# Huber loss on one core: two rows per partition in pair slots in place of one row per slot

## The chip, the cores and the metric

The kernel runs on one core of one Trainium2 chip. The time is device microseconds of one execution. Before was timed three times. One execution was taken with the hardware profiler, and all durations below are from it.

## The reference

```python
# pred, target: (8192, 8192) float32
diff = pred - target
abs_diff = np.abs(diff)
out = np.where(abs_diff <= 1.0, 0.5 * diff**2, abs_diff - 0.5)
```

It is elementwise: 256 MiB of `pred` and 256 MiB of `target` are read, 256 MiB are written, and each output element depends on one element of either input. Both kernels use the same identity: with d the difference and c the difference clamped to [0, 1] (of |d|) or [-1, 1] (of d), the result is max(|d| - 0.5, c * c / 2).

## The kernel before

The 8192 rows are cut into 64 blocks of 128 rows. A block's row p lies in partition p, so that each partition holds one whole row of 8192 float32 values, 32 KiB. Six slots of 128 x 8192 are the whole of the working memory (192 KiB in each partition), and no slot belongs to one tensor: `free` and `spent` are lists of slot numbers. A block takes one slot `a` for pred and one slot `b` for target. The result is written over the target (`b`); the pred slot is spent as soon as the block's last instruction has read it, and the target slot when its store has landed.

All loads and stores are issued from SP, in the order of the program, and a DMA that must wait for its slot holds up all that stand behind it. In steady state the order is: pred of block i (L66, into a spent slot), target of block i (L68, into the slot whose store has to land first), store of block i-2 (L73).

Five instructions compute a block. VectorE (DVE) subtracts (`sub`, L41), ScalarE (ACT) takes the absolute value in place (`absolute`, L49), DVE clamps it into the target's slot (`clamp`, L44), ACT squares that and halves it (`half_square`, L52), and DVE joins both with a maximum (`finish`, L55). The finish of a block is issued after the subtraction of the next one (`waiting`, `settle`). The last four blocks (`FINE`) are computed in four pieces of 2048 columns, and the last block's target load and the last store are cut in the same way.

The order of instructions on every engine is the one in which the program writes them (`tc.manual_schedule()`); waits follow from the tiles' data.

Of the kernel before, what the change touches and what calls it, by code (L numbers as in the profile page):

```python
# [1 line left out]

# [4 lines left out]


@with_exitstack
def kernel(  # L10
    ctx: ExitStack,
    tc: tile.TileContext,
    pred: bass.AP,
    target: bass.AP,
    out: bass.AP,
):
    nc = tc.nc
    P = 128
    fp32 = mybir.dt.float32
    Alu = mybir.AluOpType  # L20
    Act = mybir.ActivationFunctionType
    SQRT_HALF = 0.70710678118654752

    n_rows, W = pred.shape
    pred_t = pred.rearrange("(n p) m -> n p m", p=P)
    targ_t = target.rearrange("(n p) m -> n p m", p=P)
    out_t = out.rearrange("(n p) m -> n p m", p=P)
    n = pred_t.shape[0]

    NSLOT = 6  # L30
    PIECES = 4
    FINE = 4

    pool = ctx.enter_context(tc.tile_pool(name="slots", bufs=1))
    slots = [pool.tile([P, W], fp32, name=f"slot{k}") for k in range(NSLOT)]
    free = list(range(NSLOT))
    spent = []
    pending = []

    def sub(a, b):  # L40
        nc.vector.tensor_tensor(out=a, in0=a, in1=b, op=Alu.subtract)  # L41

    def clamp(a, b):
        nc.vector.tensor_scalar(  # L44
            out=b, in0=a, scalar1=0.0, scalar2=1.0, op0=Alu.max, op1=Alu.min
        )

    def absolute(a):
        nc.scalar.activation(out=a, in_=a, func=Act.Abs)  # L49

    def half_square(b):
        nc.scalar.activation(out=b, in_=b, func=Act.Square, scale=SQRT_HALF)  # L52

    def finish(a, b):
        nc.vector.scalar_tensor_tensor(  # L55
            out=b, in0=a, scalar=-0.5, in1=b, op0=Alu.add, op1=Alu.max
        )

    def cuts(pieces):
        w = W // pieces  # L60
        return [slice(k * w, (k + 1) * w) for k in range(pieces)]

    def load(i):
        ia = spent.pop(0) if i >= 3 else free.pop(0)
        ib = free.pop(0) if free else spent.pop(0)
        nc.sync.dma_start(out=slots[ia], in_=pred_t[i, :, :])  # L66
        for c in cuts(PIECES if i == n - 1 else 1):
            nc.sync.dma_start(out=slots[ib][:, c], in_=targ_t[i, :, c])  # L68
        return ia, ib

    def store(i, ib):
        for c in cuts(PIECES if i == n - 1 else 1):
            nc.sync.dma_start(out=out_t[i, :, c], in_=slots[ib][:, c])  # L73
        free.append(ib)

    ctx.enter_context(tc.manual_schedule())

    waiting = []

    def settle(keep):  # L80
        while len(waiting) > keep:
            finish(*waiting.pop(0))

    def compute(a, b, pieces):
        lag = 1 if pieces == 1 else 2
        if pieces > 1:
            while waiting and waiting[0][0].shape[1] == W:
                finish(*waiting.pop(0))
        for c in cuts(pieces):
            sub(a[:, c], b[:, c])  # L90
            absolute(a[:, c])
            settle(lag - 1)
            clamp(a[:, c], b[:, c])
            half_square(b[:, c])
            waiting.append((a[:, c], b[:, c]))

    for i in range(n):
        ia, ib = load(i)
        if i >= 2 and i < n - 1:
            store(*pending.pop(0))  # L100
        spent.append(ia)
        pending.append((i, ib))
        compute(slots[ia], slots[ib], PIECES if i >= n - FINE else 1)
    settle(0)
    for p in pending:
        store(*p)


# [1 line left out]
_INS = ['pred', 'target']  # L110
_OUTS = [((8192, 8192), 'float32')]


# [23 lines left out]
```

## Time and profile before

| | |
|---|---|
| median of 3 runs | 1873.06 us (1871.8 to 1877.19) |
| profiled execution, its own time | 1873.31 us |
| its span | 1871.5 us |
| DVE busy | 1386.8 us (74%), 228 instructions |
| ACT busy | 906.0 us (48%), 153 instructions |
| DMA packets, bytes | 28517, 805.36 MB, mean 430 GB/s |
| target load of 4 MiB, issue to landing (median) | 19.3 us |
| store of 4 MiB, issue to landing (median) | 21.4 us |
| pred load of 4 MiB, issue to landing (median) | 30.6 us |

The span runs from the first to the last event of the profiled execution; 1.8 us of the execution's own time lie around it. "Issue to landing" counts from the DMA instruction on SP to the arrival of its last byte, so it holds the time that the transfer spent in the queue behind earlier ones. In the busy tenths each digit is one of 40 equal slices of the span (46.8 us each), and 9 stands for 90% or more.

### The profile page before, as it was taken

Reading aid. Unit: us, or ns where it says so; the run is one execution under the profiler, and the core shown is the slowest. Engines: PE = TensorE matmul, PEld = TensorE weight load, DVE = VectorE, ACT = ScalarE, POOL = GpSimd, SP = SyncE. Lnnn points to the kernel's source line nnn. Section 1 sums busy time; section 2 is a strip of 40 time slices with the busy share of each in tenths; the row PEclk is TensorE's granted clock in tenths of the full one; section 3 lists DMA queues with packets and bytes.
Section 4 is the critical chain, followed back from the end, with each engine's and each line's share of the span. In section 5 each row is a group of like instructions: output and inputs, shape, how many; then the busy total and the mean of one; then the engine's idle time right before and its main releaser. Section 6 shows DMA issues by size and latency. Waiting matters only on the chain.

```text
span 1871.5 us, 823 instructions
## 1 busy us (share of the span) xinstructions
DVE 1386.8 (74%) x228; ACT 906.0 (48%) x153; POOL 0.2 (0%) x4
## 2 busy tenths in 40 slices
DVE  3886776868678687686776867768678686686787
ACT  2644545444454444544545445444454444544555
POOL 0000000000000000000000000000000000000000
DMA  9999999999999999999999999999999999999998
GB/s 415 415 432 431 432 432 429 434 426 430 435 431 434 434 431 434 433 432 434 432 432 435 431 434 432 433 434 433 432 433 434 431 435 431 434 433 432 434 434 382
DMA packets 28517, 805.36 MB, mean 430 GB/s; under 512 B 3168, under 2 KB 3168, under 8 KB 3168
## 3 DMA queue, kind: packets, MB, share of 16 engines
q1 hardware_dynamic: 28512, 805.32, 100.0%
q14 instruction: 5, 0.04, 0.0%
HBM read 536.87 MB, written 268.44 MB: 430 GB/s over the span
## 4 chain that ended last, share of the span: by engine, by line
DMA 68%; DVE 31%; ACT 0%; issue 0%; DVEq 0%; SPq 0%
DMA out_dram<-slot 35%; DMA slot<-in_target_dram 32%; DVE slot L41 15%; DVE slot L55 15%; DVE slot L44 1%; ACT slot L49 0%; DVEq L132 0%; DVEq L41 0%; SPq L66 0%; SPq L68 0%; DVEq L44 0%; SPq L73 0%
## 5 line engine op out<-in xcount | busy, mean ns | idle before, releaser
L41 DVE TENSOR_TENSOR slot<-slot,slot 128x8192 f32<-128x8192 f32 (+1 forms) x76 | 558.1, 7343 | 456.2 <-DMA slot<-in_target_dram 456.2
L49 ACT ACTIVATE slot<-slot 128x8192 f32<-128x8192 f32 (+1 forms) x76 | 452.4, 5952 | 576.3 <-DVE slot L41 576.3
L52 ACT ACTIVATE slot<-slot 128x8192 f32<-128x8192 f32 (+1 forms) x76 | 452.3, 5951 | 375.7 <-DVE slot L44 375.7
L55 DVE SCALAR_TENSOR_TENSOR slot<-slot,slot 128x8192 f32<-128x8192 f32 (+1 forms) x76 | 557.5, 7337 | 7.1 <-ACT slot L52 7.1
L44 DVE TENSOR_SCALAR slot<-slot 128x8192 f32<-128x8192 f32 (+1 forms) x76 | 284.8, 3747 | 11.0 <-ACT slot L49 11.0
L49 ACT ACT_TABLE_LOAD x1 | 1.3, 1283 | 0.7 <-PEq L121 0.7
L121 POOL MEMSET const-bfloat16-1.0<- 128x1 bf16 x1 | 0.1, 101 | 0.0
L121 POOL MEMSET const-uint8-127<- 128x1 uint8 x1 | 0.1, 101 | 0.0
L121 POOL MEMSET const-float32-0.0<- 128x1 f32 x1 | 0.1, 98 | 0.2 <-issue 0.2
L121 POOL MEMSET const-float32-1.0<- 128x1 f32 x1 | 0.1, 98 | 0.0
## 6 DMA issues: line engine op xcount, KB each, us to landing
slot<-in_pred_dram SPq DMA_DIRECT2D x64, 4096.0 KB, 30.6
slot<-in_target_dram SPq DMA_DIRECT2D x63, 4096.0 KB, 19.3
out_dram<-slot SPq DMA_DIRECT2D x63, 4096.0 KB, 21.4
slot<-in_target_dram SPq DMA_DIRECT2D x4, 1024.0 KB, 15.2
out_dram<-slot SPq DMA_DIRECT2D x4, 1024.0 KB, 9.8
```

The source lines that it names most:

```text
L41: nc.vector.tensor_tensor(out=a, in0=a, in1=b, op=Alu.subtract)
L44: nc.vector.tensor_scalar(out=b, in0=a, scalar1=0.0, scalar2=1.0, op0=Alu.max, op1=Alu.min)
L49: nc.scalar.activation(out=a, in_=a, func=Act.Abs)
L52: nc.scalar.activation(out=b, in_=b, func=Act.Square, scale=SQRT_HALF)
L55: nc.vector.scalar_tensor_tensor(out=b, in0=a, scalar=-0.5, in1=b, op0=Alu.add, op1=Alu.max)
L121: nc = _bacc.Bacc("TRN2", target_bir_lowering=False, num_devices=1)
```

## The change

A block is now 256 rows, and each partition holds two neighbouring rows of it, which lie next to each other in memory: 64 KiB. There are 32 such blocks. The same 192 KiB in each partition are laid out as two pair slots of 64 KiB (`pairs`), which alternate from block to block, and two row slots of 32 KiB (`rows`). A pair slot takes both rows of pred in one load, is computed in place, and is stored in one store. A row slot takes one row of the target: slot 0 the even rows, slot 1 the odd rows.

The order on SP in one period is: store of pair i-1, odd target row of block i, pair i+1 of pred, even target row of block i+1. The odd target row and the store both wait for the computation of block i-1's odd rows; the next pair waits for the store of the pair that had its slot; the even target row waits for the computation of block i's even rows.

A row is computed in pieces: two of 4096 columns (even), 4096, 2048 and 2048 (odd), and four of 2048 for the last block. Within a piece DVE subtracts and clamps to [-1, 1] one after the other, ACT squares and then takes the absolute value, and DVE's finish follows up to two pieces later (and writes over pred's place, not the target's). A row's pieces are all finished before the next row begins. The five operations are the same in number per element as before.

The first block's even row is loaded in four DMAs of 2 MiB, and pred's odd row of the first block and both pred rows of the last block are loaded one by one. The last block's odd target row and odd output row go in four pieces of 1 MiB.

```diff
-    NSLOT = 6
-    PIECES = 4
-    FINE = 4
-    slots = [pool.tile([P, W], fp32, name=f"slot{k}") for k in range(NSLOT)]
+    R = 2
+    pred_t = pred.rearrange("(n p r) m -> n p (r m)", p=P, r=R)
+    targ_t = target.rearrange("(n p r) m -> n p (r m)", p=P, r=R)
+    out_t = out.rearrange("(n p r) m -> n p (r m)", p=P, r=R)
+    pairs = [pool.tile([P, R * W], fp32, name=f"pair{k}") for k in range(2)]
+    rows = [pool.tile([P, W], fp32, name=f"row{k}") for k in range(R)]
+    EVEN = [4096, 4096]
+    ODD = [4096, 2048, 2048]
+    FINE = [2048, 2048, 2048, 2048]
...
+    def load_pair(i):
+        nc.sync.dma_start(out=pairs[i % 2], in_=pred_t[i, :, :])
+    def load_row(i, r, widths=None):
+        for c in cuts(widths or [W]):
+            nc.sync.dma_start(out=rows[r][:, c], in_=targ_t[i, :, at_row(r, c)])
+    def store_pair(i):
+        nc.sync.dma_start(out=out_t[i, :, :], in_=pairs[i % 2])
...
+        for c in cuts(widths):
+            a, b = pairs[i % 2][:, at_row(r, c)], rows[r][:, c]
+            nc.vector.tensor_tensor(out=a, in0=a, in1=b, op=Alu.subtract)
+            nc.vector.tensor_scalar(
+                out=b, in0=a, scalar1=-1.0, scalar2=1.0, op0=Alu.max, op1=Alu.min
+            )
+            nc.scalar.activation(out=b, in_=b, func=Act.Square, scale=SQRT_HALF)
+            nc.scalar.activation(out=a, in_=a, func=Act.Abs)
+            todo.append((a, b))
+            finish(2)
+        finish(0)
...
-    for i in range(n):
-        ia, ib = load(i)
-        if i >= 2 and i < n - 1:
-            store(*pending.pop(0))
-        spent.append(ia)
-        pending.append((i, ib))
-        compute(slots[ia], slots[ib], PIECES if i >= n - FINE else 1)
-    settle(0)
-    for p in pending:
-        store(*p)
+    for c in cuts(EVEN):
+        nc.sync.dma_start(out=pairs[0][:, c], in_=pred_t[0, :, c])
+        nc.sync.dma_start(out=rows[0][:, c], in_=targ_t[0, :, c])
+    load_pred_row(0, 1)
+    for i in range(n):
+        last = i == n - 1
+        if not last:
+            load_row(i, 1)
+            if i + 1 < n - 1:
+                load_pair(i + 1)
+            else:
+                load_pred_row(i + 1, 0)
+        compute(i, 0, EVEN if not last else FINE)
+        if not last:
+            load_row(i + 1, 0)
+        compute(i, 1, ODD if not last else FINE)
+        if i + 1 == n - 1:
+            load_pred_row(i + 1, 1)
+            load_row(i + 1, 1, FINE)
+        if not last:
+            store_pair(i)
+    store_row(n - 1, 0, [W])
+    store_row(n - 1, 1, FINE)
```

More of the change, by code (lines that the diff above doesn't have):

```diff
@@ L24 @@
     n_rows, W = pred.shape
-    pred_t = pred.rearrange("(n p) m -> n p m", p=P)
-    targ_t = target.rearrange("(n p) m -> n p m", p=P)
-    out_t = out.rearrange("(n p) m -> n p m", p=P)
+    pred_t = pred.rearrange("(n p r) m -> n p (r m)", p=P, r=R)
+    targ_t = target.rearrange("(n p r) m -> n p (r m)", p=P, r=R)
+    out_t = out.rearrange("(n p r) m -> n p (r m)", p=P, r=R)
     n = pred_t.shape[0]
-    NSLOT = 6
-    PIECES = 4
-    FINE = 4
     pool = ctx.enter_context(tc.tile_pool(name="slots", bufs=1))
-    slots = [pool.tile([P, W], fp32, name=f"slot{k}") for k in range(NSLOT)]
@@ L36 @@
[L36 to L74, printed above, removed]
@@ L76 @@
-    ctx.enter_context(tc.manual_schedule())
[L78 to L95, printed above, removed]
@@ new lines, with cuts, at_row, load_pred_row @@
+    FINE = [2048, 2048, 2048, 2048]
+    def cuts(widths):
+        out_, at = [], 0
+        for w in widths:
+            out_.append(slice(at, at + w))
+            at += w
+        return out_
+    def at_row(r, c):
+        return slice(r * W + c.start, r * W + c.stop)
+    def load_pair(i):
+        nc.sync.dma_start(out=pairs[i % 2], in_=pred_t[i, :, :])
+    def load_pred_row(i, r):
+        c = slice(r * W, (r + 1) * W)
+        nc.sync.dma_start(out=pairs[i % 2][:, c], in_=pred_t[i, :, c])
@@ new lines, in load_row, with store_row, compute, finish @@
+    def load_row(i, r, widths=None):
[3 more added lines that the diff above has]
+        nc.sync.dma_start(out=out_t[i, :, :], in_=pairs[i % 2])
+    def store_row(i, r, widths):
+        for c in cuts(widths):
+            ca = at_row(r, c)
+            nc.sync.dma_start(out=out_t[i, :, ca], in_=pairs[i % 2][:, ca])
+    def compute(i, r, widths):
+        todo = []
+        def finish(keep):
+            while len(todo) > keep:
+                a, b = todo.pop(0)
+                nc.vector.scalar_tensor_tensor(
+                    out=a, in0=a, scalar=-0.5, in1=b, op0=Alu.add, op1=Alu.max
+                )
+        for c in cuts(widths):
+            a, b = pairs[i % 2][:, at_row(r, c)], rows[r][:, c]
+            nc.vector.tensor_tensor(out=a, in0=a, in1=b, op=Alu.subtract)
+            nc.vector.tensor_scalar(
+                out=b, in0=a, scalar1=-1.0, scalar2=1.0, op0=Alu.max, op1=Alu.min
+            )
+            nc.scalar.activation(out=b, in_=b, func=Act.Square, scale=SQRT_HALF)
[3 more added lines that the diff above has]
+        finish(0)
```

## The prediction, made before the changed kernel ran

> **What bounds the kernel now.** I read the page first: busy tenths, rates, DMA queue, chain.
>
> ```profile
> DVE  3886776868678687686776867768678686686787
> ACT  2644545444454444544545445444454444544555
> DMA  9999999999999999999999999999999999999998
> GB/s 415 415 432 431 432 432 429 434 426 430 435 431 434 434 431 434 433 432 434 432 432 435 431 434 432 433 434 433 432 433 434 431 435 431 434 433 432 434 434 382
> q1 hardware_dynamic: 28512, 805.32, 100.0%
> DMA 68%; DVE 31%; ACT 0%; issue 0%; DVEq 0%; SPq 0%
> ```
>
> The DMA engines are busy in every slice. DVE has a quarter of its time free and ACT half, so DVE's 31% of the chain is not a bound: the next view shows that another transfer already lies in the queue meanwhile. The rate is 432 to 434 GB/s, but 415 in the first two slices. The bytes stay the same, so only three things can move the time: the rate, holes in the queue, and the two ends.
>
> The timeline of SP (start, length, instruction) shows the cadence. L68 is a target load, L73 a store, L66 a pred load, 4 MiB each.
>
> ```profile
> 60.14 0.35 SPq L73 DMA_DIRECT2D out_dram<-slot  x1
> 72.33 0.33 SPq L68 DMA_DIRECT2D slot<-in_target_dram  x1
> ...
> 455.83 0.33 SPq L68 DMA_DIRECT2D slot<-in_target_dram  x1
> 484.91 0.33 SPq L68 DMA_DIRECT2D slot<-in_target_dram  x1
> ...
> 513.97 0.33 SPq L68 DMA_DIRECT2D slot<-in_target_dram  x1
> 521.65 0.34 SPq L73 DMA_DIRECT2D out_dram<-slot  x1
> 522.08 0.38 SPq L66 DMA_DIRECT2D slot<-in_pred_dram  x1
> 543.02 0.33 SPq L68 DMA_DIRECT2D slot<-in_target_dram  x1
> ...
> 1705.68 0.33 SPq L68 DMA_DIRECT2D slot<-in_target_dram  x1
> ```
>
> From 484.91 to 1705.68 there are 42 periods of 29.07 us: 9.69 us for each 4 MiB, without a hole, since the pred load is still in the queue when the target load is issued on the landing of a store. From 72.33 to 484.91 there are 14 periods in 412.58 us, which is 5.7 us more than 14 x 29.07 (406.9). An empty queue shows a transfer's fixed part: the store of 60.14 lands at 72.33, 12.19 us, of which 2.5 us is not transfer. That store also came after the six first loads had run out (24 MiB, 58.1 us): a hole of 1.1 us (the landings around it, at 61.4 and 72.2, stand 10.8 apart and not 9.69).
>
> The packet records of the trace say where the 5.7 us went. A packet of 32 KiB takes 1213 ns, one of 8 KiB 309 ns: a line through both gives about 7.7 ns per packet beside the bytes. Between 79 and 485 us 145 packets of 32 KiB took over 1240 ns, and 141 of these lie in the tail of a target load, where the queue goes over to a store; after 485 us there are five. Meanwhile the sixteen DMA engines drift apart: the landings of one transfer spread over 0.3 us at 42 us, 2.9 at 357, 5.2 from 446 on, and there they stay. So the switch from load to store costs something while the engines run nearly in step (the periods that begin at 336.89, 366.31, 396.05 and 425.84 are 0.35, 0.67, 0.72 and 0.92 us too long, and that is the end of it) and nothing once they are 5.2 us apart.
>
> The sum of before: 0.73 (first issue) + 2.5 + 192 x 9.69 (1860.4) + 1.1 + 5.7 = 1870.4, and 1.1 to the end of the span of 1871.5; 1.81 lies around it (1873.31). That is 0.25 above the median of 1873.06.
>
> **The change, part by part.** The groups by form give the durations:
>
> ```profile
> L41 DVE TENSOR_TENSOR slot<-slot,slot 128x8192 f32<-128x8192 f32 x60 | 521.5, 8692 | 450.4 <-DMA slot<-in_target_dram 450.4
> L49 ACT ACTIVATE slot<-slot 128x8192 f32<-128x8192 f32 x60 | 421.8, 7030 | 555.1 <-DVE slot L41 555.1
> L44 DVE TENSOR_SCALAR slot<-slot 128x8192 f32<-128x8192 f32 x60 | 265.2, 4420 | 7.1 <-ACT slot L49 7.1
> L41 DVE TENSOR_TENSOR slot<-slot,slot 128x2048 f32<-128x2048 f32 x16 | 36.5, 2284 | 5.8 <-DMA slot<-in_target_dram 5.8
> L52 ACT ACTIVATE slot<-slot 128x2048 f32<-128x2048 f32 x16 | 30.6, 1910 | 22.6 <-DVE slot L44 22.6
> L44 DVE TENSOR_SCALAR slot<-slot 128x2048 f32<-128x2048 f32 x16 | 19.5, 1221 | 4.0 <-ACT slot L49 4.0
> ```
>
> A line through the 2048 and 8192 wide forms gives 4096 columns: subtract and finish 4.42, clamp 2.29, ACT 3.62.
>
> *Does the queue stay full?* A period of after moves 24 MiB: store pair (19.38), target row 1 (9.69), next pair (19.38), target row 0 (9.69), 58.1 us. Each issue must come 2.5 us before its predecessors land. Take t=0 as the landing of target row 1 of pair i-1; the next pair and row 0 behind it land at 19.4 and 29.07. The store behind those waits for `compute(i-1, 1)`, so it has until 26.6. DVE: subtract to 4.4, clamp 6.7, then subtract, clamp, subtract, clamp of 2048 to 13.7. ACT begins at 6.8 and ends its first two passes at 13.95, the next two at 17.6, the last at 21.4. DVE's finishes end at 18.4, 20.6 and 23.7. The new wait of each clamp for the subtract on its own engine has no row; the nearest is 0.03 from ACT to DVE, so I bound three of them by 0 and 0.3 and take 0.1. The store goes at 23.8: 2.8 us to spare. If that cover were gone, each us would cost 31 us, once per store. The other issues have more: target row 1 stands directly behind the store; the next pair waits for the store to land, with 9.7 - 2.5 = 7.2 us of row 1 left in the queue; row 0's buffer is free at -3.5, 20 us early. DVE is free again 3.5 us before t=0. DVE works 49 of 58 us with its waits. Cost: nothing.
>
> *The start.* The store of pair 0 waits for `compute(0, 1)`: row 1 of the target lands after 16 MiB (0.73 + 2.5 + 38.8 = 42.0), plus 23.8 is 65.8, while loads reach to 71. The hole of 1.1 us goes. The cut first row adds 16 packets per engine, 0.1 us.
>
> *The end.* Behind the last pair store (lands at 58 on the clock of period 30) wait one row and four pieces; the last finish comes at 70.2, its piece must be issued by 72.6. No hole; the pieces are as many as before.
>
> *Longer rows.* 30 pair loads and 31 pair stores have 64 KiB contiguous on both sides. If each partition goes as one packet, 61 x 8 packets per engine fall away: 488 x 7.7 ns = 3.8 us. If they are cut at 32 KiB, 0. A row of this trace past 32 KiB doesn't exist; I take 3.8, since 8 and 32 KiB rows both went as one packet. 139 transfers instead of 198 save nothing in themselves: back to back they stand at 9.69 us, the rate of 8 packets.
>
> The Trainium skill's page SBUF — State Buffer, "The DMA setup-cost knee", would give about 2 us per transfer, by it 59 fewer save an estimated 118 us; the back-to-back cadence above contradicts that here. Against the change speaks the page DMA: Bandwidth & Descriptors, "Latency and other measured facts": large power-of-two row pitches slow transfers, 207 against 214 GB/s at 512 KiB; were the target rows' new 64 KiB pitch to cost the same 3%, my estimate is 20 us, and no row of before has such a pitch.
>
> From this trace the pitch is bounded by nothing and by the worst long stretch, 412.58 against 406.9 us, 1.4%, on 63 row loads (610 us): 8 us. I take 0, the calm cadence.
>
> *The switch.* Load-to-store switches fall from 62 to 31. If the drift heals them after 14 as before, they cost the same 5.7, only later (by 810 us). But the drift may now be held: an engine over 2.8 us ahead finds its queue empty until the store is issued, so 5.2 us may never be reached. Bounds: 0 to 31 x 0.92 = 28 us. I take 5.7.
>
> Sum: 1873.31 - 1.1 - 3.8 + 0.1 = **1868.5 us**, 0.24% below the median.
>
> **The rivals.**
> *Held in step (slower).* The fast engines stop at 2.8 us and start each store together, and the other 17 switches cost as those near that spread did, 0.67 (0.35 to 0.92): 17 x 0.67 = 11.4, 1880 us (1874 to 1884). For it: the loss grew until 5.2 us. Against: fast engines that wait leave the slow ones alone. It is slower past 0.6 us per switch.
> *Switches nearly free.* If the early loss belongs to the first 485 us of a run, or halves with the switches, 0 to 2.9 us is left: 1863 to 1866, 1864.5.
> *Packets of 32 KiB.* The change does not give longer packets: 1868.5 + 3.8 = 1872.3.
> *Store late or pitch.* The 2.8 us are overdrawn by 0.5 us (31 x 0.5 = 15), or the pitch takes 8: 1877 to 1900.
>
> **How the numbers follow.** Forecast 0.38 (1866 to 1871), held 0.23, nearly free 0.17, short packets 0.10, late store or pitch 0.12. About 0.3% (5.6 us) is what a measurement tells from no change: faster is below 1867.4, slower above 1878.7. The forecast gives 0.17 faster and 0.21 same, nearly free 0.17 faster, short packets 0.10 same, held 0.06 same and 0.17 slower, the last 0.12 slower: 0.34, 0.37, 0.29. The range of 1863 to 1888 leaves out the best end and the long tail of the last case.
>
> **What would show it.** Right: 20,016 packets in the queue (7,808 of 64 KiB) and not 27,824; SP's pair loads 58.0 us apart in the later part; stores issued 23.8 us after target row 1 lands; an early part that is too long by some 6 us in all. Held in step: periods over 58.5 us to the end. Wrong altogether: DVE's chain of odd rows over 26 us, or periods too long from the first to the last with no switch to blame.

## The result, and the profile after

| | before | changed |
|---|---|---|
| median of 15 runs | 1872.68 us | 1877.06 us (1872.9 to 1878.79) |
| ratio of the times | | 1.0019, 95% interval 1.0012 to 1.0026 |
| profiled execution (span) | 1873.31 (1871.5) | 1877.36 (1875.6) |

The changed kernel is slower, by 0.19%. That is inside the 0.3% of the forecast's bound, and with 15 runs of each it is clear of zero. I had forecast 0.24% faster; the measured time lies in the range, the sign is wrong, and it is the rival "held in step" (1874 to 1884) that came. The time is in the range only because the rivals had stretched it upwards. Two of the 15 runs took 1872.9 and 1873.11 us, no longer than before; why, no trace shows.

The page of the changed kernel, the same parts as before, with the queue of the instructions (q14) added:

```profile
DMA  9999999999999999999999999999999999999999
GB/s 425 414 436 435 438 425 429 439 428 431 440 425 442 429 429 442 419 434 443 417 436 432 439 425 426 425 442 427 428 428 442 424 427 443 418 435 423 428 425 386
q1 hardware_dynamic: 20016, 805.32, 99.9%
q14 instruction: 9, 0.07, 0.0%
DMA 57%; ACT 24%; DVE 17%; SPq 1%; issue 0%; DVEq 0%
```

The packets are 20,016 as forecast: the 64 KiB rows went as one packet each. The DMA engines are still busy in every slice, so nothing looks like a hole, and yet the rate never settles at 433 as it did before. ACT's 24% of the chain is the odd row's computation, which the store waits for.

SP's pair loads (L50) mark the periods. From the changed kernel's timeline:

```profile
91.66 0.33 SPq L50 DMA_DIRECT2D pair<-in_pred_dram  x1
...
500.95 0.33 SPq L50 DMA_DIRECT2D pair<-in_pred_dram  x1
559.02 0.33 SPq L50 DMA_DIRECT2D pair<-in_pred_dram  x1
617.07 0.33 SPq L50 DMA_DIRECT2D pair<-in_pred_dram  x1
676.24 0.33 SPq L50 DMA_DIRECT2D pair<-in_pred_dram  x1
...
1611.15 0.33 SPq L50 DMA_DIRECT2D pair<-in_pred_dram  x1
1669.21 0.33 SPq L50 DMA_DIRECT2D pair<-in_pred_dram  x1
1728.50 0.33 SPq L50 DMA_DIRECT2D pair<-in_pred_dram  x1
```

A period is the time from one pair load to the next, and an undisturbed one is 58.06 us (559.02 to 617.07, 1611.15 to 1669.21); two periods of before are 58.13. But 28 periods from 91.66 to 1728.50 take 1636.84 us, 11.2 us more than 28 x 58.06, and 16 of them are over 0.2 us too long, up to the last one (1669.21 to 1728.50, 1.23 us too long). Before, all of it was over at 485 us. In three of the long periods a part of the excess is in the store: a fetch of instructions falls into it (660.6, 1127.9 and 1595.4 us in the packet records), and it lands 0.74 to 0.81 us late, 2.3 us together. The experiments come back to these fetches.

One period, from the timeline of the changed kernel:

```profile
1503.24 4.43 DVE L80 TENSOR_TENSOR pair<-pair,row 128x4096 f32<-128x4096 f32 x1 [3.55 <-DMA row<-in_target_dram]
1507.70 2.29 DVE L81 TENSOR_SCALAR row<-pair 128x4096 f32<-128x4096 f32 x1
...
1524.38 2.29 DVE L74 SCALAR_TENSOR_TENSOR pair<-pair,row 128x2048 f32<-128x2048 f32 x1 [0.57 <-ACT pair L85]
1526.70 0.34 SPq L61 DMA_DIRECT2D out_dram<-pair  x1
...
1533.01 4.42 DVE L80 TENSOR_TENSOR pair<-pair,row 128x4096 f32<-128x4096 f32 x1 [6.33 <-DMA row<-in_target_dram]
```

The odd target row lands at 1503.24, the store goes 23.5 us later, and the even target row of the next pair, the last load ahead of that store, lands 29.8 us after the first landing instead of 29.03, half of the calm period. That row's load is where most of the time goes: by the landings in the trace the 31 even-row loads are together 9.2 us late, up to 1.18 each. The sixteen engines' landings of one transfer spread over 3.3 us at 482 us and over 3.1 to 4.9 us from then on, and from about 740 us on some twelve of the sixteen lie within 0.3 to 1.1 us of each other (0.5 as a rule), with three or four stragglers behind them. Before, they were strung out over 5.2 us, the first twelve over 3.2.

That the leading engines are held can be read off the same landings. From 709 us on the first engine has its part of the even row in 0.7 to 2.1 us after the issue of the store (but for the last store), and its part of the store 21.1 to 21.8 us after that issue. From the one landing to the other eight packets of 2418 ns would take 19.34 us, and it took 0.2 to 1.2 us more: for so long this engine had nothing to move.

### The profile page after: what moved, and what is told of

Same layout as the page of the kernel before. It is cut to its first block, busy times and chain, and to the rows that moved or that the text cites. A ratio compares the mean times of both kernels' runs of the same rounds, so it can differ in the third digit from the quotient of the medians.

```text
span 1875.6 us, 1196 instructions
## 1 busy us (share of the span) xinstructions
DVE 1430.2 (76%) x489; ACT 912.9 (49%) x327; POOL 0.2 (0%) x4
## 3 DMA queue, kind: packets, MB, share of 16 engines
q1 hardware_dynamic: 20016, 805.32, 99.9%
## 4 chain that ended last, share of the span: by engine, by line
DMA 57%; ACT 24%; DVE 17%; SPq 1%; issue 0%; DVEq 0%
DMA row<-in_target_dram 57%; ACT row L84 12%; ACT pair L85 12%; DVE pair L80 8%; DVE pair L74 4%; DVE row L81 4%; SPq L61 1%; DVEq L140 0%; SPq L94 0%; SPq L93 0%; SPq L58 0%; SPq L54 0%; DVEq L80 0%
## 5 line engine op out<-in xcount | busy, mean ns | idle before, releaser
L84 ACT ACTIVATE row<-row 128x4096 f32<-128x4096 f32 (+1 forms) x163 | 468.4, 2874 | 948.5 <-DVE row L81 948.5
L80 DVE TENSOR_TENSOR pair<-pair,row 128x4096 f32<-128x4096 f32 (+1 forms) x163 | 571.1, 3504 | 306.7 <-DMA row<-in_target_dram 306.7
L74 DVE SCALAR_TENSOR_TENSOR pair<-pair,row 128x4096 f32<-128x4096 f32 (+1 forms) x163 | 568.7, 3507 | 122.4 <-ACT pair L85 122.4
L85 ACT ACTIVATE pair<-pair 128x4096 f32<-128x4096 f32 (+1 forms) x163 | 467.4, 2867 | 0.0
L81 DVE TENSOR_SCALAR row<-pair 128x4096 f32<-128x4096 f32 (+1 forms) x163 | 299.1, 1835 | 5.6
L84 ACT ACT_TABLE_LOAD x1 | 1.3, 1283 | 0.7 <-PEq L129 0.7
```

The costliest lines, as they stand in the source:

```text
L74: nc.vector.scalar_tensor_tensor(out=a, in0=a, scalar=-0.5, in1=b, op0=Alu.add, op1=Alu.max)
L81: nc.vector.tensor_scalar(out=b, in0=a, scalar1=-1.0, scalar2=1.0, op0=Alu.max, op1=Alu.min)
```

## The experiments

"Before" is timed beside each (1872.2 to 1872.7 us); the ratios are to it.

| | us | ratio, 95% interval |
|---|---|---|
| changed kernel | 1877.06 | 1.0019 (1.0012 to 1.0026) |
| even row's store issued early | 1871.39 | 0.9995 (0.9986 to 1.0004) |
| pair store that waits for no arithmetic (leaves the loss out) | 1871.02 | 0.9993 (0.9984 to 1.0002) |
| pair store 2 us later | 1884.33 | 1.0063 (1.0050 to 1.0075) |
| before, stores 6.7 us later | 1890.35 | 1.0095 (1.0081 to 1.0109) |
| row stores, two pieces | 1871.42 | 0.9993 (0.9984 to 1.0002) |
| row stores, eight pieces | 1881.66 | 1.0049 (1.0035 to 1.0063) |
| row stores and row loads | 1872.97 | 1.0001 (0.9992 to 1.0010) |
| row stores from ACT | 1962.67 | 1.0479 (1.0465 to 1.0493) |
| even store from ACT, odd from SP | 1880.60 | 1.0037 (1.0025 to 1.0050) |
| both from ACT, pair load split | 1905.40 | 1.0172 (1.0158 to 1.0185) |

**The even row's store on its own, ahead of the odd row's computation.**

```diff
             load_row(i + 1, 0)
+            store_row(i, 0, [W])
         compute(i, 1, ODD if not last else FINE)
...
-            store_pair(i)
+            store_row(i, 1, [W])
```

> The pair store is split into two row stores of 4 MiB, and the even row's store is issued as soon as the even row is computed, ahead of the odd row's computation. Held-store theory (in the changed kernel the store comes only 2.8 us before the slowest DMA engine needs it, so the engines that lead run dry, all start the store together, and the load-to-store switch goes on costing time to the end): the odd row's store now has 9.7 us more in the queue ahead of it, nobody is held, the landings of one transfer spread to about 5 us, the last third of the run has periods of 58.1 us without exception, and the loss at the switch is 5 to 7 us in all; with half of the long packets gone (1.9 us) some 1869 to 1872 us, 0.2 to 0.4% under the changed kernel. Rival (the pair pattern itself, 64 KiB rows and pitch, costs at each switch): losses go on through the whole run, spread below 5 us, 1875 us or more.

1871.39 us, as the held-store theory said. The odd row's store is still issued 23.5 us after its target row has landed, but the queue holds the even row's store ahead of it. The early periods are too long by up to 0.83 us (325.00 to 383.89); after 400 us only three periods are over 0.5 us too long, and in each of these an instruction fetch falls into the transfer that is late (660.1, 1097.1 and 1533.7 us; more on fetches below). The spread goes beyond the changed kernel's, to 5.7 us at 1113 us and 6.6 at the end.

**The pair store kept, and made to wait for nothing.**

```diff
-            a, b = pairs[i % 2][:, at_row(r, c)], rows[r][:, c]
+            a = b = rows[r][:, c]
```

> All five operations work on the target row alone, in the same number, size and order, so that the pair store waits for no arithmetic (its output is pred; the loss itself is left out of it). The DMAs are those of the changed kernel, packet for packet, and so is the order on SP. Held-store theory: the store is issued some 20 us earlier, no engine runs dry, the switch heals as in the kernel before, and the time falls to 1864 to 1870 us, with a spread of 5 us or more. Rival (pair pattern): as slow as the changed kernel, 1874 to 1878 us, with excess at the switches to the end.

The kernel leaves the loss out; its output is pred. 1871.02 us, 6 us under the changed kernel (5 by the ratios to before) with the very same transfers, so the pair pattern itself is not the cost; it is 1 us above the range I gave. Its pair loads:

```profile
383.57 0.33 SPq L50 DMA_DIRECT2D pair<-in_pred_dram  x1
442.29 0.33 SPq L50 DMA_DIRECT2D pair<-in_pred_dram  x1
500.37 0.33 SPq L50 DMA_DIRECT2D pair<-in_pred_dram  x1
...
674.85 0.33 SPq L50 DMA_DIRECT2D pair<-in_pred_dram  x1
733.87 0.33 SPq L50 DMA_DIRECT2D pair<-in_pred_dram  x1
791.93 0.33 SPq L50 DMA_DIRECT2D pair<-in_pred_dram  x1
...
1082.24 0.33 SPq L50 DMA_DIRECT2D pair<-in_pred_dram  x1
1140.29 0.33 SPq L50 DMA_DIRECT2D pair<-in_pred_dram  x1
```

The period from 383.57 is the last costly switch (0.66 us), at a spread of 2.7 us; then 58.06 us as a rule, as the seven periods from 733.87 to 1140.29 show (406.42 us). In the stretch from 486 to 1705 us (columns: length, busy time of DVE, ACT and POOL, clock, DMA share, GB/s) the changed kernel, the kernel before and this one stand like this, in this order:

```profile
486.00:1705.00 1219.00, 934.06 (x315) 597.65 (x210) 0.00 (x0) 1.00 1.00 431
```

```profile
486.00:1705.00 1219.00, 906.74 (x127) 588.71 (x85) 0.00 (x0) 1.00 1.00 433
```

```profile
486.00:1705.00 1219.00, 935.05 (x315) 609.22 (x210) 0.00 (x0) 1.00 1.00 433
```

431 against 433 GB/s in this stretch is where the effect shows, and it goes when the store no longer waits. The DMA share is 1.00 in all three: that column can't show it.

**The pair store 2 us later.**

```diff
-    ODD = [4096, 2048, 2048]
+    ODD = [4096, 4096]
```

> The odd row is computed in two pieces of 4096 columns instead of three, so the store of the pair is issued 25.5 us after the odd target row has landed instead of 23.5: 1.1 us to spare instead of about 3. Held-store theory: the leading engines are stopped earlier, the landings spread over 1 to 2.5 us only, and losses at the switches go on to the end; at the spread of 1 to 2 us the kernel before lost 0.2 to 0.5 us per switch, so 31 switches lose 6 to 15 us: 1872 to 1882 us. Late-store rival (what the changed kernel loses is simply a store that comes too late for the slowest engine): up to 2 us more per store, 31 x 1 to 2, so 1905 us or more. Pair-pattern rival: no change, 1877 us.

1884.33 us, 7 us over the changed kernel and 2 us over my upper end. From its timeline (landing of the odd row, store, landing of the even row):

```profile
1329.90 4.43 DVE L80 TENSOR_TENSOR pair<-pair,row 128x4096 f32<-128x4096 f32 x1 [3.55 <-DMA row<-in_target_dram]
...
1355.31 0.34 SPq L61 DMA_DIRECT2D out_dram<-pair  x1
...
1360.56 4.43 DVE L80 TENSOR_TENSOR pair<-pair,row 128x4096 f32<-128x4096 f32 x1 [5.28 <-DMA row<-in_target_dram]
```

The store goes 25.4 us after the landing and the even row lands after 30.7: 1.6 us late in this period. The spread is held at 1.6 to 3.3 us from 560 us on, and 22 of 28 periods are over 0.2 us too long (16.2 us in all, against 11.2 with the store 2 us earlier). It is not the 31 to 62 us of a store that simply comes too late.

**The kernel before, with late stores.**

```diff
+    idle = [pool.tile([P, 2000], fp32, name=f"idle{k}") for k in range(2)]
...
+            for _ in range(fill):
+                nc.vector.tensor_tensor(
+                    out=idle[1], in0=idle[0], in1=idle[0], op=Alu.subtract
+                )
             settle(lag - 1)
```

`fill` is 3 for the blocks 4 to 59.

> The kernel before, with three idle subtractions of 2000 columns on DVE (6.7 us) put ahead of the finish in blocks 4 to 59, so that each store is issued some 24 us after the target load has landed instead of 17.4: about 2.4 us to spare instead of 9.2. Tiles, packets and order of the DMAs are those of before. Held-store theory: the spread of the landings stays near 2.5 to 4 us instead of 5.2, and the switch goes on costing 0.2 to 0.7 us each to the end instead of nothing after 485 us: 48 further switches, 10 to 30 us, so 1883 to 1903 us. Rival (the early loss belongs to the start of a run, or the loss of the changed kernel to its pairs): 1873 us as before, with a calm cadence after 485 us.

1890.35 us, 18 us over before. Its timeline:

```profile
1004.27 8.69 DVE L42 TENSOR_TENSOR slot<-slot,slot 128x8192 f32<-128x8192 f32 x1 [0.74 <-DMA slot<-in_target_dram]
1012.88 6.79 DVE L96 TENSOR_TENSOR idle<-idle 128x2000 f32<-128x2000 f32 x3
...
1028.29 0.34 SPq L74 DMA_DIRECT2D out_dram<-slot  x1
...
1033.84 8.69 DVE L42 TENSOR_TENSOR slot<-slot,slot 128x8192 f32<-128x8192 f32 x1 [1.24 <-DMA slot<-in_target_dram]
```

The store goes 24.0 us after the landing, and the next target row lands after 29.6 us instead of 29.07, still at 1000 us. The spread stays at 2.7 to 4.3 us from 540 us on, with a median engine 0.2 to 0.3 us behind the first, as in the changed kernel. Single rows, no pairs, half as many bytes a store: the late store brings the loss without them. That the added DVE work itself slows the transfers is the obvious rival, and the landings speak against it: of the 18 us some 15 fall on the target loads, the last ahead of each store, 2 to 3 on the stores and 0.5 on the pred loads, while the idle subtractions run from 8.6 to 15.4 us after a target landing, where a store ends and a pred load moves.

**Row stores, the odd row in two pieces.** The first experiment, with the edit of the third.

> The row stores of the experiment before, with the odd row computed in two pieces of 4096 columns instead of three. The odd row's store then comes 2 us later, but it still has about 10 us to spare. Held-store theory: no change in the switch, 1869 to 1872 us, while the same two pieces with a pair store gave 1884; fewer instructions (12 instead of 15 DVE and 8 instead of 10 ACT in a pair) may take one of the instruction fetches with them that land on the slowest DMA engine (0.8 to 1 us each). Late-store rival: 1873 us or more, since each odd row is finished later.

1871.42 us. What cost 7 us with a pair store costs nothing once 4 MiB stand in the queue ahead. The fetches were not fewer: four of the periods or rows that came 0.6 to 1 us late coincide with one, as in the first experiment.

**Row stores, every row in eight pieces.**

```diff
-    ODD = [4096, 2048, 2048]
+    ODD = [1024] * 8
...
-        compute(i, 0, EVEN if not last else FINE)
+        compute(i, 0, ODD if not last else FINE)
```

> The row stores with every row computed in eight pieces of 1024 columns (24 DVE and 16 ACT instructions a row; DVE's work grows to about 52 of 58 us and the finish of a row still ends under 26 us after its landing). Fetch theory (isolated periods that are 0.8 to 1 us too long are instruction fetches that share a DMA engine with the data): two to three times as many instruction packets in the queue of the instructions, and 4 to 8 such periods instead of 3, so 1 to 5 us more than with three pieces: 1872 to 1876 us. Rival (the isolated periods have another cause): 1871 us, three of them.

1881.66 us, more than I expected. Its queue of the instructions:

```profile
q14 instruction: 23, 0.19, 0.0%
```

23 packets of 8 KiB instead of 9. In the trace's packet records 11 of them are followed, a few us later, by a landing that is 0.8 to 1 us late, and the spread of the engines jumps by about as much; with three pieces it was 4 of 9, 0.3 to 1 us each. They stand about 150 us apart here. They may be the fetches of DVE's instructions, of which there are 1512 here and 489 there, but no run tells DVE's from ACT's. The direction of the fetch theory holds, its size was too low. From 1050 us on there is also loss without a fetch, at a spread of 7 to 8.7 us: there the next pair load, which is issued some 7.2 us ahead of need, is the issue that holds the leading engines: its first part lands 21.2 to 21.5 us after its issue (1145.17, 1262.96 and 1381.76), as with the held stores. No run tests that by moving it.

**Row stores and row loads.**

```diff
-        nc.sync.dma_start(out=pairs[i % 2], in_=pred_t[i, :, :])
+        load_pred_row(i, 0)
+        load_pred_row(i, 1)
```

> The row stores, and each pair load split in two row loads of 4 MiB, so that no packet is longer than 32 KiB; every transfer now has the pitch of 64 KiB. Packet theory: 24,800 or so packets, a calm cadence of 58.14 us instead of 58.08, 1.9 us in all: 1873 us. Pitch rival: rows with the 64 KiB pitch are slower than whole pairs by more than that, a calm cadence over 58.3 us and 1878 us or more. No-effect rival: 58.08 us and 1871 us.

1872.97 us and a calm cadence of 58.15 us, against 1871.4 (first and fifth experiment) and 58.06 to 58.1 with pair loads. That is near what the packet theory gave, 0.06 us a period and 1.9 in all; the pitch of 64 KiB costs nothing that shows. (The queue had 28,800 packets; the count in the expectation was miscounted.)

**The stores from ACT.** Three arrangements:

```diff
-            nc.sync.dma_start(out=out_t[i, :, ca], in_=pairs[i % 2][:, ca])
+            nc.scalar.dma_start(out=out_t[i, :, ca], in_=pairs[i % 2][:, ca])
```

> The row stores are issued from ACT instead of SP, at the same place of the program, so that they stand in a queue of their own beside the loads. Theory (what costs is that engines in step all go over from load to store at the same moment): with two queues loads and stores alternate all the time, there is no such moment, the excess of the first 500 us goes and 1865 to 1869 us result. Rival (reading and writing at the same time costs in itself, and a switch is dear because it mixes them): the mixed stretches are slow from the first to the last, over 1875 us.

1962.67 us. Windows of this kernel, with both queues loaded and then with SP waiting for the odd store:

```profile
602.00:625.00 23.00, 22.06 (x10) 14.32 (x6) 0.00 (x0) 1.00 1.00 433
625.00:649.00 24.00, 18.74 (x7) 14.14 (x4) 0.00 (x0) 1.00 0.90 371
649.00:653.00 4.00, 4.00 (x1) 0.00 (x0) 0.00 (x0) 1.00 0.78 262
```

With both queues loaded it is 433 GB/s: reading and writing at once costs nothing that shows in this stretch, which speaks against the rival's reason. But the store and the loads share the engines, the odd store lands together with the row beside it, and the pair load that waits for it finds an empty queue. The time lies on the rival's side, but for another reason than it gave.

The even store alone from ACT (`store_row(i, 0, [W], nc.scalar)`):

> The row stores again, but only the even row's store is issued from ACT; the odd row's store stays on SP behind the loads. The experiment with both stores on ACT moved 433 GB/s while both queues had work and lost its time with empty queues, because the next pair waits for an odd store that lands no sooner than everything else; here the odd store keeps the loads ahead of it. Same-moment theory: half of each store is spread over the loads, the engines go over to the odd store from a mixture and not from pure loads, the switch costs less than with both on SP, nothing runs dry: 1866 to 1870 us. Rival (the odd store's switch is as dear as before): 1871 to 1872 us. Rival (the even store delays the next pair and its row by up to 9.7 us and the queue runs dry): 1890 us or more.

1880.60 us, outside all three ranges: 28 periods are 12.5 us too long (6.4 with both stores on SP), and the last 98 us run at 394 GB/s (401 with both on SP), which is some 2 us more. Both stores from ACT, the pair load split:

```diff
+            load_pred_row(i + 1, 0)
             load_row(i, 1)
-            if i + 1 < n - 1:
-                load_pair(i + 1)
-            else:
-                load_pred_row(i + 1, 0)
+            load_pred_row(i + 1, 1)
...
```

> Both row stores on ACT, and each pair load split in two row loads that wait for the store of their own half alone, the first of them ahead of the odd target row, so that a load is always queued when the odd store lands. No switch is left in either queue. Same-moment theory: no excess but the instruction fetches, landings within 1 to 2 us of each other, calm cadence 58.15 us (all packets 32 KiB): 1866 to 1870 us. Rival (empty queues, as with the unsplit pair): 1890 to 1960 us, with a rate of 433 GB/s wherever both queues have work.

1905.40 us: from 600 to 1200 us it runs at 431 GB/s and the 29 periods from 106.64 to 1799.36 are 6.4 us longer in all than 29 x 58.15. The largest part of the loss, some 15 us, stands at the end: the last 41 us run at 205 GB/s, where the row stores from SP have 362. The rival's range was met, not mine, but its empty queues show at the end. These three show that a second queue is no remedy here; whether the loss at a switch comes of its being at one moment they leave open.

## Why the prediction was wrong

The profiled execution took 1877.36 us and the forecast was 1868.5, 8.9 us apart. By its terms:

- **The step that failed: the switch.** "If the drift heals them after 14 as before, they cost the same 5.7": it did not heal them. The store that waits for the odd row's last finish holds every engine that is some 3 us ahead, and those engines then start the store together. The pair store without that wait is 6.1 us faster in its profiled execution (1871.26), and that is the size of this step; instruction fetches take about as much in both (2.3 and 2.7 us) and don't make the difference. That the late store causes the loss is shown from both sides: without the wait the loss goes, a late store put into the kernel before makes one of 18 us, and a store 2 us later makes it grow. I had written this mechanism down with 2.8 us of slack and weighed it at 0.23; the argument that I set against it ("fast engines that wait leave the slow ones alone") was argued from no measurement and was wrong: where the leaders are held, the last engine comes late too.
- **The slack itself was right.** 23.8 us from landing to store forecast, 23.5 measured. "Cost: nothing" was read off the slowest engine. For an engine whose lead is larger than the slack it is a wait.
- **The packets.** Number and length were right, 488 fewer per engine. A packet of 64 KiB takes 2418 ns, two of 32 KiB 2426. By these 16 packets fewer in a period would make 0.13 us. The term was mis-sized all the same: the calm period fell from 58.13 to 58.06 us, 0.07 a period, which is 2.2 us in 31 periods and not 3.8: 1.6 us of the miss. Why only half of the packets' time shows is open.
- **The rest, 1.2 us** (6.1, 1.6 and 1.2 make the 8.9). The forecast counted 5.7 us of losses at the switch and no others. By the same sum the pair store without the wait loses 6.9 in all: 2.7 in three periods that hold an instruction fetch (674.85 to 733.87 is 0.96 too long), 2.3 in the other periods after 92 us, most of it at switches, and the remainder, 1.9, at both ends. That the whole comes near 5.7 is luck: the switches took less, and the fetches, which had no term, took as much.
- **The start.** The hole of 1.1 us went, but the first switch, with all engines in step, is 0.95 us late in its place.
- **The two rules weighed.** The Trainium skill's page SBUF — State Buffer, "The DMA setup-cost knee", has 2 us per transfer: with 59 transfers fewer the calm cadence moved by 0.07 us in 58, so the trace decides against it in a queue that is full. Its page DMA: Bandwidth & Descriptors, "Latency and other measured facts", warns of row pitches of 512 KiB and more: at 64 KiB a period takes 58.15 us with the pitch on every transfer and 58.13 before without it, no cost that shows; pitches of 512 KiB no run here has.

Of the rivals, "held in step" gave 1880 and the mechanism; its price was too high, 0.67 for each of 17 switches, where the 31 even-row loads lost 0.30 on average. "Switches nearly free" was half right: undisturbed, they cost about 2.3 us after the first and all but stop with the seventh store, at 442 us, where before it took 14 periods, to 485 us. That is nearer to this rival's "first 485 us of a run" than to the forecast's count of 14.

What stays open is why a switch costs time at all, and why the last engine loses where the leaders are held. Mixing alone does not explain it (433 GB/s with both queues loaded), and the stores from ACT did not show that the common moment is what counts. Nor is it enough that the leaders are close together: at 1350 us, in the kernels with row stores and with the free pair store, the first eleven of the sixteen lie within 0.7 to 1 us and nothing is lost, in the changed kernel within 0.4 and the loss goes on.

## What to carry to other kernels

In a queue that is always full, measure the slack of each issue against the lead of the fastest DMA engine, not against the slowest: an issue that comes 2.5 to 3 us ahead of need cost 6 us here, with 31 stores, and 18 us where it came up 56 times, while every engine counted as busy. A large store that waits for the last of a large computation is better cut, so that its first half stands in the queue while the second is computed: that gave back all that the late pair store had cost. None of these versions is clearly faster than the kernel before; the best that computes the loss (row stores, odd row in two pieces) is at 0.9993 with an interval that reaches past 1.

## What the runs showed of the hardware that was not expected

- The sixteen DMA engines of one queue don't stay together. Undisturbed they drift apart by 5.2 to 6.6 us, in before and with the row stores or the free pair store. The losses at the switches had all but ended at a spread of 2.6 to 3.9 us with the latter, and at 5.2 in before; in the changed kernel, where the leaders are held, they went on at 3.5 to 4.8.
- A fetch of instructions (8 KiB, 9 in runs of 1196 and 1283 instructions, 23 with 2997) can delay the landing of a transfer by 0.3 to 1 us. That it falls on the engine that is last is inferred: the first landings are on time, and the spread grows by as much. A cut into more pieces pays for that too: of the 10 us that eight pieces cost over three, seven more such fetches make up an estimated 6 to 7.
- Loads and stores in two queues at once moved 433 GB/s from 602 to 625 us of one run, as much as one queue with loads and stores in turn, and 429 to 431 from 80 to 1780 us of another.
